# A conditioned hybrid decoder layer on one core: x in four loads, factor products spread out, five tiles of x1 turned by a transpose, and seven constant matmuls

## The chip, the core and the metric

The kernel runs on one NeuronCore of a Trainium2 chip. The metric is the device time of one execution in microseconds (us), the median of several runs; lower is better. One more execution was recorded by the hardware profiler, and all durations below come from it.

The engines are named as the profile names them: PE (matmul), PEld (its weight loads), DVE (vector), ACT (activation), POOL, and SP, which here only issues loads. Each works through its own list of instructions in order and waits at an instruction until what it needs is there.

## What is computed

One decoder layer for 256 tokens of width 2048 and a final norm, all in float32, with weights of some 380 MB read once:

```
mod = silu(c) W_ada + b_ada -> shift1, scale1, gate1, shift2, scale2, gate2
h   = RMSNorm(x)(1+scale1)+shift1
p   = h W_in                        (12288 columns: retention, HGRN2, two branch gates)
yA  = W_retO( LN_head(Retention(rope(q),rope(k),v)) * silu(g) )
yB  = W_hgO( RMS_head(HGRN2(silu(q), f, i)) * silu(g) )
x   = x + gate1 * ( (sigmoid(gA)*yA + sigmoid(gB)*yB) W_out )
h2  = RMSNorm(x)(1+scale2)+shift2
u   = causal_depthwise_conv3(h2 W_up) ; [a, b] = split(u)
x   = x + gate2 * ( (silu(a) * b) W_down )
out = RMSNorm_final(x)
```

## The kernel before

**Products.** A float32 weight piece of two k-tiles (128 x 1024, 512 KB) is loaded into `raw` (12 buffers), ACT copies its upper part to `wh` (`upper`, L165), DVE subtracts to get the lower part `wl` (`rest`, L170); both have four buffers. Activations are split alike: `hT` and `h2T` hold 256 upper and 256 lower columns for each k-tile. PE then forms hi x hi, lo x hi and hi x lo.

**The start (0 to about 43 us).** `load_x` (L268) brings x transposed in eight loads of 256 KB on SP's queue. `norm_x` (L312) squares them, two on DVE and six on ACT, with the four silu of c between ACT's squares, and adds them up on DVE. `token_rstd` (L282) sums over partitions with PE, takes the square root on ACT and the reciprocal on DVE, and spreads the result `rx` with two more matmuls. For each k-tile `scale_shift` (L386) makes scale and shift of the norm by four long products on DVE (`ada_dot`, L380: 1024 columns of W_ada times `sc`, summed). `times` (L367) multiplies x by `rx` in place; `modulated` (L337) makes the upper half of `hT` on ACT, the same value again as `h` on ACT, and the lower half by a subtraction on DVE. `run` does this by hand for the k-tiles 0 and 1, against four groups of columns (FIRST), and hands the other 14 to a background list (`ada[2:]`), from which `pump` takes steps in proportion to the products issued. Their seven `times` (512 columns each, k = 2, 4, ... 14) are tied only to an early instruction called `start`.

**Order.** Where `self.ordered` holds, `pin` keeps instructions in the order of the program text. Elsewhere a scheduler settles the order when the kernel is built. Either way each engine's list is fixed before the run.

**From x1 to h2T (about 785 to 822 us).** After the last group of W_out, `residual` (L875) adds to x1 and squares it, `row_rstd` (L893) gives a factor `rr` for each row, and `diag` (128 x 128) gets the factors on its diagonal. `turn_rows` (L345) multiplies 128 x 128 blocks of x1 by `diag` on PE, which turns and scales them at once. A tile of 512 columns holds two k-tiles of both row halves. The tiles j = 0, 1, 2 are turned first; `act2` (L852) turns j = 3 to 7 later, each ahead of the products that come one pair of k-tiles before its own. `modulated2` (L352) makes two k-tiles of `h2T` out of a tile in PSUM: on ACT the upper half of the first k-tile, `h` of the first, the upper half of the second; on DVE `h` of the second, then both subtractions. Then `up_group` (L900) runs the products with W_up: for each k-tile four matmuls of 512 columns (L913) and four of 256 (L915). One weight piece of W_up is prepared ahead of the last `residual`.

Of the kernel before, what the change touches and what calls it, by code (L numbers as in the profile page):

```python
# [55 lines left out]
class Kernel:  # L56
# [172 lines left out]
    def constants(self):  # L229
        nc, a, c = self.nc, self.a, self.consts  # L230
        self.ones = c.tile([P, P], F32, name="ones")
        nc.vector.memset(self.ones, 1.0)
        self.eps1 = c.tile([P, 1], F32, name="eps1")
        nc.vector.memset(self.eps1, NORM_EPS)
        self.eps2 = c.tile([P, 1], F32, name="eps2")
        nc.vector.memset(self.eps2, HEAD_EPS)
        self.halfpi = c.tile([P, 1], F32, name="halfpi")
        nc.vector.memset(self.halfpi, math.pi / 2)

        self.silu = []  # L240
        self.sc = c.tile([P, D + 1], F32, name="sc")
        nc.vector.memset(self.sc[:, D:], 1.0)
        rows = [self.blk([1, GW], name="crow") for _ in range(2)]
        for u, row in enumerate(rows):
            nc.scalar.dma_start(out=row, in_=a["c"][:, u * GW : (u + 1) * GW])
        self.small_loads(nc.scalar, ("ident", "gn1"))
        for u in range(4):
            at = slice(u * G, (u + 1) * G)
            ps = self.po()
            nc.tensor.matmul(ps, lhsT=self.ones[0:1, :], rhs=rows[u // 2][:, u % 2 * G : (u % 2 + 1) * G], start=True, stop=True)  # L250
            self.silu.append((self.sc[:, at], ps))

    def small_loads(self, engine, names):
        for name in names:
# [13 lines left out]
    def load_x(self):  # L268

        out = [self.blk([P, 4, T], name="xT") for _ in range(4)]  # L270
        for i in range(8):
            u = slice(i % 2 * 2, i % 2 * 2 + 2)
            self.pin(self.nc.sync.dma_start(out=out[i // 2][:, u, :], in_=self.a["xT"][:, 2 * i : 2 * i + 2, :]))
        return out

    def load_rows(self, j):
# [5 lines left out]
    def token_rstd(self, parts):  # L282


        nc = self.nc
        ps = self.po()[:, :NT]
        for i, z in enumerate(parts):
            for t in range(NT):

                nc.tensor.matmul(  # L290
                    ps[:, t : t + 1],
                    lhsT=z[:, t * P : (t + 1) * P],
                    rhs=self.ones[:, 0:1],
                    start=i == t == 0,
                    stop=i == len(parts) - 1,
                    skip_group_check=True,
                )
        q = self.small([P, NT], name="rq")
        nc.scalar.activation(q, ps, AF.Sqrt, bias=self.eps1, scale=1.0 / D)
        self.pin(nc.vector.reciprocal(q, q))  # L300

        ps = self.po()[:, :T]
        for t in range(NT):
            nc.tensor.matmul(ps[:, t * P : (t + 1) * P], lhsT=q[:, t : t + 1].to_broadcast([P, P]), rhs=self.ident, start=True, stop=True)
        return ps

    def sqrt_table(self):
# [4 lines left out]
    def norm_x(self):  # L312

        nc = self.nc
        self.xT = self.load_x()
        parts = []
        for i in range(8):
            x = self.xT[i // 2][:, i % 2 * 2 : i % 2 * 2 + 2, :]
            z = self.s2([P, 2, T], name="sq")
            if i < 2:  # L320
                nc.vector.tensor_tensor(z, x, x, ALU.mult)
            else:
                if self.silu:
                    self.pin(nc.scalar.activation(*self.silu.pop(0), AF.Silu))
                self.pin(nc.scalar.activation(z, x, AF.Square))
            if i % 2:
                nc.vector.tensor_tensor(z, z, last, ALU.add)
                if i % 4 == 3:
                    nc.vector.tensor_tensor(z[:, 0, :], z[:, 0, :], z[:, 1, :], ALU.add)
                    parts.append(z[:, 0, :])  # L330
                else:
                    parts += [z[:, 0, :], z[:, 1, :]]
            last = z
        self.sqrt_table()
        return parts

    def modulated(self, dst, x, k, sc, sh):  # L337

        act = self.nc.scalar.activation
        h = self.s1([P, T], name="h")  # L340
        self.pin(act(dst[:, :T], x, AF.Identity, bias=sh[:, k : k + 1], scale=sc[:, k : k + 1]))
        self.pin(act(h, x, AF.Identity, bias=sh[:, k : k + 1], scale=sc[:, k : k + 1]))
        self.pin(self.nc.vector.tensor_tensor(dst[:, T:], h, dst[:, :T].bitcast(F32), ALU.subtract))

    def turn_rows(self, ps, x, k, diag, t):  # L345

        for i in range(2):
            cols = slice((k + i) % 4 * P, ((k + i) % 4 + 1) * P)
            at = slice((NT * i + t) * P, (NT * i + t + 1) * P)
            self.pin(self.nc.tensor.matmul(ps[:, at], lhsT=x[k // 4][:, t, cols], rhs=diag[:, t, :], start=True, stop=True))  # L350

    def modulated2(self, dst, ps, k, sc, sh):  # L352

        nc = self.nc
        z = ps.rearrange("p (j t) -> p j t", j=2)
        hs = [self.s1([P, T], name="h") for _ in range(2)]
        for i, h in enumerate(hs):
            j = k + i
            self.pin(nc.scalar.activation(dst[:, i, :T], z[:, i, :], AF.Identity, bias=sh[:, j : j + 1], scale=sc[:, j : j + 1]))
            if i:  # L360
                self.pin(nc.vector.tensor_scalar(h, z[:, i, :], sc[:, j : j + 1], sh[:, j : j + 1], ALU.mult, ALU.add))
            else:
                self.pin(nc.scalar.activation(h, z[:, i, :], AF.Identity, bias=sh[:, j : j + 1], scale=sc[:, j : j + 1]))  # L363
        for i, h in enumerate(hs):
            self.pin(nc.vector.tensor_tensor(dst[:, i, T:], h, dst[:, i, :T].bitcast(F32), ALU.subtract))  # L365

    def times(self, k, n, r):  # L367
# [289 lines left out]
    def run(self):  # L657
# [12 lines left out]
        def act(k):  # L670
            return hT[k // 2][:, k % 2, :]

        def ada1(k):
            yield from self.scale_shift("ada1", k, s1, t1, self.gn1)
            if k % 2 == 0:
                hT[k // 2] = self.blk([P, 2, 2 * T], F32R, name="hT")
                if k:
                    ins = self.times(k, 2, rx_sb)
                    self.tc.add_manual_dep(ins.ins, start.ins.name, NOSYNC, reason="after the start")
            self.modulated(act(k), self.xT[k // 4][:, k % 4, :], k, s1, t1)  # L680
            yield 0.7

# [11 lines left out]


        ada = [ada1(k) for k in range(KT)]
        for _ in range(2):
            next(ada[0])
        rx = self.token_rstd(parts)
        rx_sb = c.tile([P, T], F32, name="rx_sb")  # L700
        ps = [self.po2(), self.po2(), self.pg(), self.pg()][:FIRST]
        for k in range(2):
            for i in range(4 if k else 2):
                if i == 1:
                    self.times(k, 1, rx)
                next(ada[k])
            part = self.upper(a["wa"][0][:, k : k + 1, :], 1, G)
            for _ in ada[k]:
                pass
            for g in range(FIRST):  # L710
                wh, wl = self.rest(part if g == 0 else self.upper(a["wa"][g][:, k : k + 1, :], 1, G))
                if k == 0:
                    start = self.last
                if k == g == 0:
                    self.pin(nc.scalar.activation(rx_sb, rx, AF.Copy))
                mms[g](ps[g], act(k), wh[:, 0, :], wl[:, 0, :], k == 0, k == 1 and g >= RESIDENT)
# [109 lines left out]
        for j in range(4):  # L826
# [4 lines left out]
            if last:  # L831
                self.finish(ada2)
                up = self.pieces(a["wup"][0], KT)
                up = chain([next(up)], up)
                self.ordered = True
            if last:
                diag = self.s1([P, NT, P], name="diag")
            for t in range(NT):
                self.residual(x1[j], ps, g, ss, j, t)
                if last:  # L840
                    r = self.row_rstd(ss, part, t)
                    self.pin(nc.vector.tensor_scalar(diag[:, t, :], self.ident, r, None, ALU.mult))
            if j == 2:
                part = self.row_part(ss)
# [6 lines left out]

        def act2(k):  # L852

            while len(h2T) < KT // 2 and 2 * len(h2T) <= k + 2:
                j = len(h2T)
                if j >= len(turned):
                    turned.append(self.po())
                    for t in range(NT):
                        self.turn_rows(turned[j], x1, 2 * j, diag, t)
                h2T.append(self.blk([P, 2, 2 * T], F32R, name="h2T"))  # L860
                self.modulated2(h2T[j], turned[j], 2 * j, self.sc2, self.sh2)
            return h2T[k // 2][:, k % 2, :]
# [206 lines left out]
```

## Time and profile before

| what | value |
|---|---|
| runs | 1540.33, 1540.42, 1541.73 us; median 1540.42 |
| profiled execution | 1540.23 us |
| its span, first to last instruction | 1538.3 us |
| outside the span | 1.9 us |
| mean granted PE clock | 0.999 |
| read from HBM | 382 MB, 250 GB/s over the span |

How to read it: the span is cut into stretches of time, and for each the profile tells how long every engine was busy. In a stretch where PE is busy all the time, nothing else can shorten the time but less work for PE. Where PE was idle, the table of waits tells what ended its idle time.

### The profile page before, as it was taken

Reading aid. Unit: us, or ns where it says so; the run is one execution under the profiler, and the core shown is the slowest. Engines: PE = TensorE matmul, PEld = TensorE weight load, DVE = VectorE, ACT = ScalarE, POOL = GpSimd, SP = SyncE. Lnnn points to the kernel's source line nnn. Section 1 sums busy time; section 2 is a strip of 40 time slices with the busy share of each in tenths; the row PEclk is TensorE's granted clock in tenths of the full one; section 3 lists DMA queues with packets and bytes.
Section 4 is the critical chain, followed back from the end, with each engine's and each line's share of the span. In section 5 each row is a group of like instructions: output and inputs, shape, how many; then the busy total and the mean of one; then the engine's idle time right before and its main releaser. Section 6 shows DMA issues by size and latency. Waiting matters only on the chain.

```text
span 1538.3 us, 22200 instructions
## 1 busy us (share of the span) xinstructions
PE 1516.6 (99%) x8286; PEld 1308.0 (85%) x8286; DVE 1173.4 (76%) x1595; ACT 843.4 (55%) x1201; POOL 4.0 (0%) x8
## 2 busy tenths in 40 slices
PE   7999999999999999999999999999999999999997
PEld 6999999888888888888878888888888888888886
DVE  7899986897998977898757787777778769455454
ACT  5755454766865554445446555555555558444343
POOL 0000000000000000000000000000000000000000
PEclk9999999999999999999999999999999999999999
DMA  9999997687777789989946777777777766677651
GB/s 362 346 345 329 319 330 228 232 280 256 247 246 261 262 293 322 320 303 342 337 121 216 226 232 233 240 222 239 230 231 232 226 189 190 206 207 206 198 166 55
DMA packets 111568, 385.69 MB, mean 251 GB/s; under 512 B 12866, under 2 KB 13410, under 8 KB 111460
## 3 DMA queue, kind: packets, MB, share of 16 engines
q1 hardware_dynamic: 110592, 383.14, 76.0%
q8 instruction: 65, 1.06, 0.3%
q10 hardware_dynamic: 868, 1.13, 0.2%
q14 instruction: 43, 0.35, 0.1%
HBM read 382.11 MB, written 2.11 MB: 250 GB/s over the span
## 4 chain that ended last, share of the span: by engine, by line
PE 94%; DVE 3%; ACT 2%; DMA 1%; issue 1%; DVEq 0%; ACTq 0%
PE pg L188 13%; PE pg L187 13%; PE pg L189 13%; PE po L913 11%; PE pg L913 10%; PE po L915 5%; PE pg L915 5%; PE po L189 3%; PE po L188 3%; PE po L187 3%; PE pg L202 3%; PE pg L200 3%; PE pg L201 3%; PE po L556 1%; DVE raw L380 1%; PE po L200 1%
## 5 line engine op out<-in xcount | busy, mean ns | idle before, releaser
L170 DVE TENSOR_TENSOR wl<-raw,wh 128x1024 fp32r<-128x1024 f32 (+1 forms) x536 | 635.0, 1189 | 283.3 <-ACT wh L165 281.9
L165 ACT ACTIVATE wh<-raw 128x1024 fp32r<-128x1024 f32 (+1 forms) x536 | 550.9, 1033 | 529.9 <-PE pg L189 190.4
L380 DVE SCALAR_TENSOR_TENSOR raw<-raw,sc 128x1024 f32<-128x1024 f32 x192 | 233.2, 1217 | 0.0
L913 PE MATMUL pg<-h2T,wh 128*128 128x512 f32 x704 | 221.6, 396 | 1.7 <-DVE h2T L365 1.7
L913 PE MATMUL po<-h2T,wh 128*128 128x512 f32 x704 | 221.2, 395 | 0.2 <-ACT wh L165 0.2
L187 PE MATMUL pg<-wh,hT 128*128 128x512 f32 x512 | 202.6, 396 | 0.0
L188 PE MATMUL pg<-wl,hT 128*128 128x512 f32 x512 | 200.2, 391 | 0.7 <-DVE wl L170 0.7
L189 PE MATMUL pg<-wh,hT 128*128 128x512 f32 x512 | 199.8, 390 | 0.0
L915 PEld LDWEIGHTS pg<-h2T,wl 128*128 128x128 f32 x704 | 131.9, 188 | 31.7 <-DVE wl L170 0.8
L915 PEld LDWEIGHTS po<-h2T,wl 128*128 128x128 f32 x704 | 132.2, 188 | 31.1
L915 PE MATMUL pg<-h2T,wl 128*128 128x256 f32 x704 | 138.5, 278 | 0.0
L915 PE MATMUL po<-h2T,wl 128*128 128x256 f32 x704 | 138.3, 278 | 0.0
L188 PEld LDWEIGHTS pg<-wl,hT 128*128 128x128 f32 x512 | 96.3, 188 | 21.1 <-DVE wl L170 2.3
L189 PEld LDWEIGHTS pg<-wh,hT 128*128 128x128 f32 x512 | 96.1, 188 | 20.2
L187 PEld LDWEIGHTS pg<-wh,hT 128*128 128x128 f32 x512 | 96.2, 188 | 19.1
L202 PE MATMUL pg<-hT,wl 128*128 128x256 f32 x384 | 109.0, 284 | 0.8 <-DVE wl L170 0.8
L200 PE MATMUL pg<-hT,wh 128*128 128x256 f32 x384 | 109.3, 285 | 0.1
L201 PE MATMUL pg<-hT,wh 128*128 128x256 f32 x384 | 109.0, 284 | 0.0
L913 PEld LDWEIGHTS pg<-h2T,wh 128*128 128x128 f32 x704 | 107.2, 189 | 1.8 <-ACT h L363 1.8
L913 PEld LDWEIGHTS po<-h2T,wh 128*128 128x128 f32 x704 | 107.2, 189 | 0.7 <-ACT wh L165 0.6
L200 PEld LDWEIGHTS pg<-hT,wh 128*128 128x128 f32 x384 | 74.1, 193 | 0.9 <-ACT wh L165 0.6
L202 PEld LDWEIGHTS pg<-hT,wl 128*128 128x128 f32 x384 | 74.0, 193 | 1.0 <-DVE wl L170 1.0
(222 smaller groups left out, 2198.4 us busy)
## 6 DMA issues: line engine op xcount, KB each, us to landing
raw<-in_wup SPq DMA_DIRECT2D x176, 512.0 KB, 4.5
raw<-in_wdown SPq DMA_DIRECT2D x88, 512.0 KB, 3.6
raw<-in_wa SPq DMA_DIRECT2D x80, 512.0 KB, 5.6
raw<-in_ada SPq DMA_DIRECT2D x64, 512.5 KB, 5.6
raw<-in_ada SPq DMA_DIRECT2D x64, 512.0 KB, 5.7
raw<-in_wab SPq DMA_DIRECT2D x64, 512.0 KB, 4.8
raw<-in_gate SPq DMA_DIRECT2D x32, 512.5 KB, 4.9
raw<-in_wb SPq DMA_DIRECT2D x32, 512.0 KB, 5.2
```

The source lines that it names most:

```text
L165: self.pin(self.nc.scalar.activation(wh, raw, AF.Copy))
L170: self.last = self.nc.vector.tensor_tensor(wl, raw, wh.bitcast(F32), ALU.subtract)
L187: nc.tensor.matmul(ps[t], lhsT=hi, rhs=wh, start=first, stop=False)
L188: nc.tensor.matmul(ps[t], lhsT=hi, rhs=wl, start=False, stop=False)
L189: nc.tensor.matmul(ps[t], lhsT=lo, rhs=wh, start=False, stop=last)
L200: nc.tensor.matmul(out, lhsT=wh[:, cs], rhs=hi, start=opens, stop=False, skip_group_check=True)
L201: nc.tensor.matmul(out, lhsT=wh[:, cs], rhs=lo, start=False, stop=False, skip_group_check=True)
L202: nc.tensor.matmul(out, lhsT=wl[:, cs], rhs=hi, start=False, stop=last, skip_group_check=True)
L380: dot = self.pin(nc.vector.scalar_tensor_tensor(raw[:, 0, :], raw[:, 0, :], 1.0, self.sc[:, u * GW : u * GW + w], ALU.mult, ALU.mult, accu ...
L556: nc.tensor.matmul(ps[:, j * 64 : (j + 1) * 64], lhsT=(kt if n > 1 else k)[:, h, c * P : (c + 1) * P], rhs=eq[:, j * 64 : (j + 1) * 64], s ...
L913: self.pin(nc.tensor.matmul(ps[j + z], lhsT=wh[:, cs[z]], rhs=act, start=kt == 0, stop=False))
L915: nc.tensor.matmul(ps[j + z][:, :T], lhsT=wl[:, cs[z]], rhs=act[:, :T], start=False, stop=kt == KT - 1)
```

## The change

**Start.** x comes in four loads of 512 KB. The first is squared on DVE, the other three on ACT in one instruction each, into buffers of a larger pool; two silu now come behind the last square. For k = 0 `modulated` makes `h` on DVE. The seven `times` of the background list stand at the head of a pair's steps and are tied to the newest `rest` (`self.last`). Matmuls of a block of ones in bfloat16 (`keep_busy`, 512 columns each) stand between steps of PE: two among the matmuls that spread c, three behind the sums of squares, two behind the spreading of `rx`.

**x1.** The tiles j = 0, 1, 2 are still turned with `diag`. For j = 3 to 7 DVE first scales x1 by the row factors into `xs` (two instructions of 256 columns), and four PE transposes turn `xs` (`turn_scaled`). `act2` does this one pair of k-tiles earlier. In `modulated2` DVE's `h` belongs to the first k-tile, ACT's to the second. Two weight pieces of W_up are prepared ahead, not one.

```
@@ constants
+        self.busy = self.sb.tile([P, G], BF16, name="busy", tag="k1", bufs=7)
+        nc.gpsimd.memset(self.busy, 1.0)
+        self.spare = self.pg()[0]
...
+            if u == 2:
+                self.keep_busy(2)
...
+    def keep_busy(self, n):
+
+        for _ in range(n):
+            self.pin(self.nc.tensor.matmul(self.spare, lhsT=self.busy[:, :P], rhs=self.busy, start=True, stop=True))
@@ load_x
-        for i in range(8):
-            u = slice(i % 2 * 2, i % 2 * 2 + 2)
-            self.pin(self.nc.sync.dma_start(out=out[i // 2][:, u, :], in_=self.a["xT"][:, 2 * i : 2 * i + 2, :]))
+        for i, z in enumerate(out):
+            self.pin(self.nc.sync.dma_start(out=z, in_=self.a["xT"][:, 4 * i : 4 * i + 4, :]))
@@ modulated
-        self.pin(act(h, x, AF.Identity, bias=sh[:, k : k + 1], scale=sc[:, k : k + 1]))
+        if k == 0:
+            self.pin(self.nc.vector.tensor_scalar(h, x, sc[:, k : k + 1], sh[:, k : k + 1], ALU.mult, ALU.add))
+        else:
+            self.pin(act(h, x, AF.Identity, bias=sh[:, k : k + 1], scale=sc[:, k : k + 1]))
@@ turn_scaled, new
+        z = self.s2([P, NT, 2 * P], name="xs")
+        for t in range(NT):
+            self.pin(self.nc.vector.tensor_scalar(z[:, t, :], x[:, t, :], rs[t], None, ALU.mult))
+        for t in range(NT):
+            for i in range(2):
+                at = slice((NT * i + t) * P, (NT * i + t + 1) * P)
+                self.pin(self.nc.tensor.transpose(ps[:, at], z[:, t, i * P : (i + 1) * P], self.ident))
@@ modulated2
             if i:
+                self.pin(nc.scalar.activation(h, z[:, i, :], AF.Identity, bias=sh[:, j : j + 1], scale=sc[:, j : j + 1]))
+            else:
                 self.pin(nc.vector.tensor_scalar(h, z[:, i, :], sc[:, j : j + 1], sh[:, j : j + 1], ALU.mult, ALU.add))
-            else:
-                self.pin(nc.scalar.activation(h, z[:, i, :], AF.Identity, bias=sh[:, j : j + 1], scale=sc[:, j : j + 1]))
-        for i, h in enumerate(hs):
             self.pin(nc.vector.tensor_tensor(dst[:, i, T:], h, dst[:, i, :T].bitcast(F32), ALU.subtract))
@@ ada1
+            if k > 0 and k % 2 == 0:
+                ins = self.times(k, 2, rx_sb)
+                self.tc.add_manual_dep(ins.ins, self.last.ins.name, NOSYNC, reason="behind the weights traced ahead of it")
...
-                if k:
-                    ins = self.times(k, 2, rx_sb)
-                    self.tc.add_manual_dep(ins.ins, start.ins.name, NOSYNC, reason="after the start")
@@ W_out, last group
-                up = chain([next(up)], up)
+                up = chain([next(up), next(up)], up)
@@ act2
-            while len(h2T) < KT // 2 and 2 * len(h2T) <= k + 2:
+            while len(h2T) < KT // 2 and 2 * len(h2T) <= k + 4:
...
-                    for t in range(NT):
-                        self.turn_rows(turned[j], x1, 2 * j, diag, t)
+                    self.turn_scaled(turned[j], x1[j // 2][:, :, j % 2 * 2 * P : (j % 2 + 1) * 2 * P], rs)
```

What this does to the engines' lists is seen at three places. The line numbers in rows of the changed kernel are its own.

DVE between the products for k = 1 and the first piece of a new group (`dot` is a long product, `xT<-xT,rx_sb` a `times`, `wl` a lower weight part). Before:

```order
L380 SCALAR_TENSOR_TENSOR raw_284,dot_283<-raw_284,sc 128x1024
L370 TENSOR_TENSOR xT_95<-xT_95,rx_sb 128x512
L380 SCALAR_TENSOR_TENSOR raw_287,dot_283<-raw_287,sc 128x1025
L370 TENSOR_TENSOR xT_96<-xT_96,rx_sb 128x512 x2
L370 TENSOR_TENSOR xT_97<-xT_97,rx_sb 128x512
L343 TENSOR_TENSOR hT_200<-h_296,hT_200 128x256
L170 TENSOR_TENSOR wl_293<-raw_290,wh_292 128x512
```

and changed:

```order
L399 SCALAR_TENSOR_TENSOR raw_280,dot_279<-raw_280,sc 128x1024
L399 SCALAR_TENSOR_TENSOR raw_283,dot_279<-raw_283,sc 128x1025
L353 TENSOR_TENSOR hT_196<-h_292,hT_196 128x256
L170 TENSOR_TENSOR wl_289<-raw_286,wh_288 128x512
L170 TENSOR_TENSOR wl_312<-raw_309,wh_311 128x512
```

The four `times` have left this place; one comes ahead of the long products for k = 2, the other six later, one ahead of each pair's products.

ACT a little later, where the first group beyond the first six begins (`p<-pg` takes a finished PSUM pair, `t` is the shift for k = 2, `wh_435` before and `wh_431` changed is that new group's first piece). Before:

```order
L392 ACTIVATE s_135<-gn_85,s_135 128x1
L165 ACTIVATE wh_435<-raw_433 128x1024
L691 ACTIVATE p_144<-pg_393 128x1024
L394 ACTIVATE t_136<-dot_418 128x1
L165 ACTIVATE wh_465<-raw_463 128x512
L341 ACTIVATE hT_426<-xT_95,t_136,s_135 128x256
L342 ACTIVATE h_428<-xT_95,t_136,s_135 128x256
```

and changed:

```order
L411 ACTIVATE s_130<-gn_88,s_130 128x1
L413 ACTIVATE t_131<-dot_415 128x1
L710 ACTIVATE p_139<-pg_390 128x1024
L348 ACTIVATE hT_423<-xT_100,t_131,s_130 128x256
L352 ACTIVATE h_424<-xT_100,t_131,s_130 128x256
L165 ACTIVATE wh_431<-raw_429 128x1024
```

The new group's first piece moved behind the taking of the last PSUM pair and behind `hT` and `h` of k = 2.

DVE from x1 to h2T, at the tiles j = 3 and 4 (`po_7461` and `po_7497` before, `po_7435` and `po_7474` changed, are those tiles in PSUM). Before:

```order
L361 TENSOR_SCALAR h_7468<-po_7461,sc_137,sh_138 128x256
L365 TENSOR_TENSOR h2T_7466<-h_7467,h2T_7466 128x256
L365 TENSOR_TENSOR h2T_7466<-h_7468,h2T_7466 128x256
L170 TENSOR_TENSOR wl_7494<-raw_7491,wh_7493 128x1024
L361 TENSOR_SCALAR h_7504<-po_7497,sc_137,sh_138 128x256
```

and changed:

```order
L384 TENSOR_TENSOR h2T_7410<-h_7412,h2T_7410 128x256
L366 TENSOR_SCALAR xs_7436<-xr_6827,rr_7361 128x256
L366 TENSOR_SCALAR xs_7436<-xr_6827,rr_7370 128x256
L383 TENSOR_SCALAR h_7444<-po_7435,sc_132,sh_133 128x256
L384 TENSOR_TENSOR h2T_7443<-h_7444,h2T_7443 128x256
L384 TENSOR_TENSOR h2T_7443<-h_7445,h2T_7443 128x256
L170 TENSOR_TENSOR wl_7471<-raw_7468,wh_7470 128x1024
L366 TENSOR_SCALAR xs_7475<-xr_7009,rr_7361 128x256
L366 TENSOR_SCALAR xs_7475<-xr_7009,rr_7370 128x256
L383 TENSOR_SCALAR h_7483<-po_7474,sc_132,sh_133 128x256
```

The scaling for the tile j = 4 now stands in DVE's list behind the subtractions of the tile j = 3 and behind the weight piece for the k-tiles 4 and 5 (`wl_7471`). The scaling for j = 3 stands behind the subtractions of j = 2. On PE the four transposes of j = 3 stand ahead of the products of k = 2, those of j = 4 ahead of k = 4, and so on to j = 7 ahead of k = 10; before, `turn_rows` for j = 3 stood ahead of k = 4, and for j = 7 ahead of k = 12.

More of the change, by code (lines that the diff above doesn't have):

```diff
@@ L249, in constants @@
             ps = self.po()
-            nc.tensor.matmul(ps, lhsT=self.ones[0:1, :], rhs=rows[u // 2][:, u % 2 * G : (u % 2 + 1) * G], start=True, stop=True)
+            if u == 2:
+                self.keep_busy(2)
+            self.pin(nc.tensor.matmul(ps, lhsT=self.ones[0:1, :], rhs=rows[u // 2][:, u % 2 * G : (u % 2 + 1) * G], start=True, stop=True))
             self.silu.append((self.sc[:, at], ps))
+    def keep_busy(self, n):
+        for _ in range(n):
+            self.pin(self.nc.tensor.matmul(self.spare, lhsT=self.busy[:, :P], rhs=self.busy, start=True, stop=True))
     def small_loads(self, engine, names):
@@ L288, in token_rstd @@
             for t in range(NT):
-                nc.tensor.matmul(
+                self.pin(nc.tensor.matmul(
                     ps[:, t : t + 1],
@@ L296, in token_rstd @@
                     skip_group_check=True,
-                )
+                ))
+        self.keep_busy(3)
         q = self.small([P, NT], name="rq")
@@ L303, in token_rstd @@
         for t in range(NT):
-            nc.tensor.matmul(ps[:, t * P : (t + 1) * P], lhsT=q[:, t : t + 1].to_broadcast([P, P]), rhs=self.ident, start=True, stop=True)
+            self.pin(nc.tensor.matmul(ps[:, t * P : (t + 1) * P], lhsT=q[:, t : t + 1].to_broadcast([P, P]), rhs=self.ident, start=True, stop=True))
+        self.keep_busy(2)
         return ps
@@ L316, in norm_x @@
         parts = []
[L317 to L321, printed above, removed]
+        for i, x in enumerate(self.xT):
+            z = self.blk([P, 4, T], name="sq")
+            if i == 0:
+                self.pin(nc.vector.tensor_tensor(z, x, x, ALU.mult))
             else:
-                if self.silu:
+                if i < 3:
                     self.pin(nc.scalar.activation(*self.silu.pop(0), AF.Silu))
                 self.pin(nc.scalar.activation(z, x, AF.Square))
[L326 to L330, printed above, removed]
-                else:
-                    parts += [z[:, 0, :], z[:, 1, :]]
-            last = z
+            self.pin(nc.vector.tensor_tensor(z[:, :2, :], z[:, :2, :], z[:, 2:, :], ALU.add))
+            self.pin(nc.vector.tensor_tensor(z[:, 0, :], z[:, 0, :], z[:, 1, :], ALU.add))
+            parts.append(z[:, 0, :])
+        for part in self.silu:
+            self.pin(nc.scalar.activation(*part, AF.Silu))
         self.sqrt_table()
@@ L350, in turn_rows, with turn_scaled @@
             self.pin(self.nc.tensor.matmul(ps[:, at], lhsT=x[k // 4][:, t, cols], rhs=diag[:, t, :], start=True, stop=True))
+    def turn_scaled(self, ps, x, rs):
+        z = self.s2([P, NT, 2 * P], name="xs")
[5 more added lines that the diff above has]
+                self.pin(self.nc.tensor.transpose(ps[:, at], z[:, t, i * P : (i + 1) * P], self.ident))
     def modulated2(self, dst, ps, k, sc, sh):
@@ L360, in modulated2 @@
             if i:
+                self.pin(nc.scalar.activation(h, z[:, i, :], AF.Identity, bias=sh[:, j : j + 1], scale=sc[:, j : j + 1]))
+            else:
                 self.pin(nc.vector.tensor_scalar(h, z[:, i, :], sc[:, j : j + 1], sh[:, j : j + 1], ALU.mult, ALU.add))
-            else:
-                self.pin(nc.scalar.activation(h, z[:, i, :], AF.Identity, bias=sh[:, j : j + 1], scale=sc[:, j : j + 1]))
-        for i, h in enumerate(hs):
             self.pin(nc.vector.tensor_tensor(dst[:, i, T:], h, dst[:, i, :T].bitcast(F32), ALU.subtract))
@@ L696, in run @@
         ada = [ada1(k) for k in range(KT)]
-        for _ in range(2):
+        for _ in range(3):
             next(ada[0])
@@ L702, in run @@
         for k in range(2):
-            for i in range(4 if k else 2):
-                if i == 1:
+            for i in range(4 if k else 1):
+                if k and i == 1:
                     self.times(k, 1, rx)
                 next(ada[k])
+            if k == 0:
+                self.times(k, 1, rx)
             part = self.upper(a["wa"][0][:, k : k + 1, :], 1, G)
@@ L711, in run @@
                 wh, wl = self.rest(part if g == 0 else self.upper(a["wa"][g][:, k : k + 1, :], 1, G))
-                if k == 0:
-                    start = self.last
                 if k == g == 0:
@@ L837, in run @@
                 diag = self.s1([P, NT, P], name="diag")
+                rs = []
             for t in range(NT):
@@ L841, in run @@
                     r = self.row_rstd(ss, part, t)
+                    rs.append(r)
                     self.pin(nc.vector.tensor_scalar(diag[:, t, :], self.ident, r, None, ALU.mult))
```

## The prediction

> **What bounds the kernel now.** I read the page first, then the span cut into stretches, then the waits of PE, then the rows of time where PE waits. The page's head and its first list:
>
> ```profile
> span 1538.3 us, 22200 instructions
> ...
> PE 1516.6 (99%) x8286; PEld 1308.0 (85%) x8286; DVE 1173.4 (76%) x1595; ACT 843.4 (55%) x1201; POOL 4.0 (0%) x8
> ```
>
> The stretches give the start, the length and the busy time of PE, PEld, DVE, ACT and POOL in that order, then the granted clock, the DMA share and GB/s:
>
> ```profile
> 0.00:14.00 14.00, 11.55 (x29) 6.95 (x30) 5.42 (x14) 8.18 (x13) 0.20 (x4) 1.00 0.88 297
> 14.00:42.00 28.00, 22.50 (x128) 20.24 (x128) 26.33 (x45) 15.42 (x29) 0.00 (x0) 1.00 1.03 401
> 42.00:500.00 458.00, 456.42 (x2890) 409.48 (x2890) 399.44 (x531) 278.07 (x397) 3.83 (x4) 1.00 0.83 284
> 500.00:766.00 266.00, 266.00 (x1211) 220.58 (x1210) 217.14 (x272) 134.15 (x180) 0.00 (x0) 1.00 0.91 313
> 766.00:830.00 64.00, 60.41 (x336) 51.30 (x335) 40.20 (x64) 38.35 (x63) 0.00 (x0) 1.00 0.49 152
> 830.00:1480.00 650.00, 650.00 (x3482) 558.66 (x3481) 459.22 (x644) 349.83 (x500) 0.00 (x0) 1.00 0.72 219
> ```
>
> PE is the bound, with hardly a gap from 42 to 766 and from 830 to 1480. There only less work for PE could help, and the change takes none away. So only two places count: the start, where DVE is busy 26.33 of the 28 us from 14 to 42, and the passage from x1 to h2T, where PE idles 3.59 us between 766 and 830. PE never catches up later on: what it loses at one of these places is lost for good, and what it gains is kept. PE's waits between 786 and 830 (the engine and line that waited, what for, us in total, times, longest):
>
> ```profile
> PE pg L913 <- DVE h2T L365: 1.7, 1, 1.7
> PE po L350 <- DVE diag L842: 1.3, 1, 1.3
> ```
>
> Both lie ahead of the first product of W_up. After it, the five later `turn_rows` cost PE their own work and almost no waiting.
>
> **From x1 to h2T: the term that decides.** Rows of time of before (start, duration, engine, line, operation):
>
> ```profile
> 791.84 0.56 ACT L359 ACTIVATE h2T<-po,sh,sc 128x256 fp32r<-128x256 f32 x1 [1.32 <-PE po L350]
> ...
> 793.81 0.75 DVE L365 TENSOR_TENSOR h2T<-h,h2T 128x256 fp32r<-128x256 f32 x2
> ...
> 794.37 0.70 PE L913 MATMUL pg<-h2T,wh 128*128 128x512 f32 x2 [1.68 <-DVE h2T L365]
> ...
> 795.85 1.22 DVE L170 TENSOR_TENSOR wl<-raw,wh 128x1024 fp32r<-128x1024 f32 x1
> ...
> 797.03 0.54 DVE L361 TENSOR_SCALAR h<-po,sc,sh 128x256 f32<-128x256 f32 x1
> ...
> 800.02 1.06 PE L350 MATMUL po<-diag,xr 128*128 128x128 f32 x8
> 800.83 0.71 PE L913 MATMUL pg<-h2T,wh 128*128 128x512 f32 x2
> 801.11 0.56 ACT L359 ACTIVATE h2T<-po,sh,sc 128x256 fp32r<-128x256 f32 x1 [3.17 <-PE po L350]
> ...
> 801.58 0.55 ACT L363 ACTIVATE h<-po,sh,sc 128x256 f32<-128x256 f32 x1
> ...
> 802.03 0.56 ACT L359 ACTIVATE h2T<-po,sh,sc 128x256 fp32r<-128x256 f32 x1
> ...
> 802.48 1.06 ACT L165 ACTIVATE wh<-raw 128x1024 fp32r<-128x1024 f32 x1
> 802.62 0.55 DVE L361 TENSOR_SCALAR h<-po,sc,sh 128x256 f32<-128x256 f32 x1 [3.24 <-ACT h2T L359]
> ...
> 815.70 0.71 PE L913 MATMUL pg<-h2T,wh 128*128 128x512 f32 x2
> ```
>
> PE's own price: 794.37 to 800.02 is four k-tiles, 1.41 each. A turn takes 0.81 (800.02 to 800.83). From 800.83 to 815.70 are four turns and eight k-tiles, 3.72 a loop, so before hardly waits.
>
> The new order of `modulated2` has the two engines hand one PSUM tile over: ACT `h2T`, DVE `h`, ACT `h2T`, ACT `h`. In before, DVE's `h` starts at 802.62, 0.03 after ACT's second `h2T` ends (802.59): a reader on the other engine waits for the first. I take the same for ACT's second `h2T` behind DVE's `h`. Then a tile holds ACT for 0.59 + 0.57 + 0.46 + 0.46 = 2.08, against 1.37 before (801.11 to 802.48). Before shows the wait in this one direction only. The Trainium skill, "PSUM — Partial Sum Buffer", section "PSUM bank collisions raise a hardware error", says that the compiler orders any two instructions of different engines on the same bank and partitions, reads against reads too. By that rule the new order pays 0.57 more per tile, as I have it; without it the change would be some 4.5 us cheaper (the third rival's sum, made from the rows).
>
> Start: the first `h` is on DVE at 791.84 + 0.59 and done by 792.89, the subtraction 0.56 later (793.81 to 794.37 is that step): the first product comes at 793.45, a gain of 0.92. Two k-tiles then keep PE to 796.27, and there stand, new, the transposes of j = 3.
>
> They need `xs`, which stands in DVE's list behind the subtractions of j = 2. That tile's ACT work starts at 791.84 + 2 x 2.08 = 796.00, its `h` on ACT ends 1.62 later, the subtraction, priced by 793.81 (0.75 for two), ends near 798.25. Transposes and scaling are priced by like rows elsewhere, four transposes on PE and a scaling of 512 columns on DVE:
>
> ```profile
> 669.36 0.60 PE L469 MATMUL po<-ident,gt 128*128 128x128 f32 x4
> ...
> 669.71 0.48 PE L187 MATMUL pg<-wh,og 128*128 128x512 f32 x1
> ...
> 1527.31 1.28 DVE L977 TENSOR_SCALAR xr<-xr,rr 128x512 f32<-128x512 f32 x3
> ```
>
> Transposes: 0.35 for four. Scaling: 0.40 from one to the next at 512 columns (three in 1.28); at 256 I estimate 0.27, between 0.20 and 0.40. So the second `xs` ends near 798.9 and the transposes start at 798.98: PE has waited 2.7 us.
>
> The loop from one tile's last transposes to the next's is then a circle through three engines: transposes to ACT 0.45, `h2T` 0.59, DVE's `h` 0.57, ACT's `h2T` 0.46 and `h` 0.46, then ACT's `wh` 1.09 (802.48), DVE's `wl` 1.18 (795.85 to 797.03), first `xs` 0.27, second `xs` to PE 0.43. Sum 5.50. PE has only 2 x 1.41 + 0.35 = 3.17 for it, so it waits 2.3 a loop; before had 3.72 and no such circle, since `turn_rows` read x1 and a `diag` long finished. Four loops bring the transposes of j = 7 to 798.98 + 22.0 = 820.98; with them and k = 10, 11 done, 824.15. The weights for k = 12, 13 are late too: `wl` is there 4.85 after the transposes, PE wants it at 3.17 + 0.47: 1.2 more. The same point of the work in before is 815.70. **Sum: 825.35 - 815.70 = +9.65** for this part, 8.0 if the estimates of `xs` and of the first tiles are all favourable, 11.5 with each step 0.1 longer. The five lighter turns save PE 5 x 0.46 = 2.3 of work, already in the sum, but PE waits there anyway. The second prepared piece of W_up is counted at nothing: ACT and DVE are free ahead of the residual; without that cover it would be 1.1 + 1.2.
>
> **The start.** The loads of x, from issue to landing, in before:
>
> ```profile
> DMA to landing us min/median/max: 3.0/5.2/6.3
> ```
>
> Rows of time of before: a square on ACT, two early products on PE, three of the four rows that hold the seven `times` on DVE, and the end of the first six groups:
>
> ```profile
> 11.44 1.15 ACT L325 ACTIVATE sq<-xT 128x512 f32<-128x512 f32 x2 [0.68 <-PE po L290]
> ...
> 24.57 0.41 PE L200 MATMUL pg<-hT,wh 128*128 128x256 f32 x1
> 24.79 0.41 PE L201 MATMUL pg<-hT,wh 128*128 128x256 f32 x1
> ...
> 27.03 0.68 DVE L370 TENSOR_TENSOR xT<-xT,rx_sb 128x512 f32<-128x512 f32 x1
> ...
> 28.78 1.88 DVE L370 TENSOR_TENSOR xT<-xT,rx_sb 128x512 f32<-128x512 f32 x3
> ...
> 36.24 1.28 DVE L370 TENSOR_TENSOR xT<-xT,rx_sb 128x512 f32<-128x512 f32 x2
> ...
> 40.98 1.04 ACT L165 ACTIVATE wh<-raw 128x1024 fp32r<-128x1024 f32 x1
> ...
> 42.08 0.39 PE L200 MATMUL pg<-hT,wh 128*128 128x256 f32 x1
> ...
> 42.16 1.02 ACT L691 ACTIVATE p<-pg 128x1024 f32<-128x1024 f32 x1
> ...
> 43.79 0.59 ACT L341 ACTIVATE hT<-xT,t,s 128x256 fp32r<-128x256 f32 x1
> ...
> 44.28 0.59 ACT L342 ACTIVATE h<-xT,t,s 128x256 f32<-128x256 f32 x1
> ```
>
> Six of the seven `times` leave DVE's chain, 0.60 each (36.24): 3.6, less 0.3 for the `h` it takes over. Earlier squares may add 0 to 2.5 (two silu of 0.6 now stand behind them on ACT, but both ahead of the square root that follows): the 0.68 wait for a buffer goes, but x is the same bytes in four loads as in eight on SP's queue, and their landing (3.0 to 6.3 us after issue) bounds the rest. I take the end of the six groups 3.7 earlier than 42.08, between 1.5 and 5.8. But the next group's first piece now stands on ACT behind `p` (1.02), `hT` and `h` (0.49 each, 43.79 to 44.28) and takes 1.04 itself: 3.04 of PE idle, where before had that piece from 40.98. Net -0.65. The six `times` that come later cost +0.15, between 0 and 0.3: from 42 to 500 DVE is busy 399 of 458 us, so there is slack to take 3.6. **Sum: -0.5**, from -2.8 to +1.5. The constant matmuls: 24.57 to 24.79 is 0.22 for 256 columns, against 1.41/12 = 0.12 in the later k-tiles, so PE is slow until about 26, though the granted clock reads 1.00. From the first products at about 20 on that is 6/0.22, some 27 of them, so a fast PE would save up to 27 x 0.10 = 2.6 of its work, but DVE's long products set `hT` for k = 1; I count 0. The Trainium skill, "TensorE: Matmul & The Clock Gate", Part 1, asks for about 3.4 us of sustained work before the clock opens. Seven such matmuls, in three pieces, are by its rule too short (an estimate: 7 x 0.43 = 3.0), so the sum by it is the same 0.
>
> **Sum.** 1540.23 - 0.5 + 9.65 = 1549.4 for a profiled execution; the median of the runs is 0.2 above it, so 1549.6.
>
> **Rivals.** *The scaled blocks never hold PE up* (faster): then the first product's 0.92 and five turns at 0.46 are gained, with 0.5 of the start: 1540.4 - 3.7 = 1536.7. It speaks for it that ACT is busy 38 and DVE 40 of 64 us: there is room on average. Against it, `xs` stands in line behind `wl`, and `wl` behind ACT's `wh`. It decides at a loop of 3.17; I have 5.50. Chance 0.06.
>
> *The clock falls while PE waits*: at 0.215 per 256 columns a k-tile takes 2.58, a loop 5.8, and k = 10 to 13 some 4 more: about 1554.5. Against it, the waits of 1.3 and 1.7 left the granted clock of 766 to 830 at 1.00, and those I forecast are up to 2.7. Chance 0.05.
>
> *ACT and DVE read the tile at once*: 0.57 less in three first tiles, four loops and the end, 4.5 in all: 1545.1. Against it the 0.03 at 802.62. Chance 0.06.
>
> *The change does less than it says after x1 and more at the start*: that last case, with the start at its best end and a PE that the constant matmuls make fast: 1545.1 - 2.3 - 2.6 = 1540.2. Chance 0.03.
>
> **How the numbers follow.** The forecast keeps 0.80. Its own range is 1540.4 + 8.0 - 2.8 = 1545.6 to 1540.4 + 11.5 + 1.5 = 1553.4, ends that need all at once; with the third rival at the lower end I give 1545.0 to 1553.0. About 0.2% (3 us) is what a measurement can tell from no change: faster is the first rival, 0.06; same the last, 0.03; slower the rest, 0.91.
>
> **What would show it.** In the profile after, PE's waits for a transpose on `xs` should total about 12 us in five pieces (the first near 2.7, the others near 2.3), ACT's second `h2T` should start about 0.03 after DVE's `h` ends, and the first product of W_up should come 0.9 sooner after the first turn's end. At the start, `wh` of the seventh group should hold PE about 3 us. I am wrong if PE is busy through the first group of W_up, if `xs` starts before `wl`, or if ACT's and DVE's reads overlap.

## The result and the profile after

The changed kernel is slower: 1552.06 us (median of 5 runs, 1550.63 to 1552.31) against 1540.42; ratio 1.0069, 95% interval 1.0058 to 1.0081. The profiled execution took 1552.06 us, its span 1550.2 against 1538.3 before: 11.9 us longer. The stretches of the changed kernel, cut as before but with the passage from x1 to h2T 12 us longer (PE, PEld, DVE, ACT, POOL busy, granted clock, DMA share, GB/s):

```profile
14.00:42.00 28.00, 23.09 (x132) 19.57 (x131) 20.86 (x37) 15.65 (x30) 0.00 (x0) 0.94 1.03 407
42.00:500.00 458.00, 455.14 (x2879) 409.07 (x2880) 400.49 (x528) 276.70 (x388) 3.83 (x4) 1.00 0.83 281
...
766.00:842.00 76.00, 64.89 (x328) 54.07 (x327) 46.82 (x75) 40.27 (x65) 0.00 (x0) 0.96 0.45 141
842.00:1492.00 650.00, 650.00 (x3482) 558.55 (x3481) 459.13 (x644) 349.73 (x499) 0.00 (x0) 1.00 0.71 219
```

The row of 766 to 842 carries most of it. From 842 on PE is busy all of 650 us with 3482 matmuls, the row of 830 to 1480 of before, 12 us later. Where 64 us stood, 76 stand now, and PE is idle 11.1 us in them instead of 3.6. Some 2.3 of these 12 us come from the start: the first turn behind the second `diag` begins that much later (rows below). In 14 to 42 DVE is down from 26.33 to 20.86 us busy, so the start did unload DVE, and the granted clock is 0.94. The waits of PE over the whole execution:

```profile
PE po L370 <- DVE xs L366: 7.5, 5, 2.4
PE pg L200 <- ACT wh L165: 3.0, 1, 3.0
PE po L200 <- ACT hT L348: 2.7, 2, 2.4
...
PE pg L935 <- DVE wl L170: 0.5, 1, 0.5
...
PE pg L933 <- ACT wh L165: 0.4, 1, 0.4
```

The two top waits are those forecast: five for `xs`, and one of 3.0 for the seventh group's first piece. The five add up to 7.5 us, though, where about 12 had been forecast. Two of them are only 0.5, because PE ran slowly ahead of them (below). The other three are 2.39, 2.07 and 2.05, where 2.7 and 2.3 had been forecast: the profile counts a wait from the end of the last product, some 0.2 later than PE could have begun the next one, and the loop itself is as long as forecast. One turn of the circle, from the transposes of one tile to the next, in the rows of time of the changed kernel:

```profile
806.81 0.63 PE L370 MATMUL po<-ident,xs 128*128 128x128 f32 x4 [0.49 <-DVE xs L366]
...
807.48 0.57 ACT L379 ACTIVATE h2T<-po,sh,sc 128x256 fp32r<-128x256 f32 x1 [2.33 <-PE po L370]
...
808.08 0.54 DVE L383 TENSOR_SCALAR h<-po,sc,sh 128x256 f32<-128x256 f32 x1 [1.15 <-ACT h2T L379]
...
808.66 0.57 ACT L379 ACTIVATE h2T<-po,sh,sc 128x256 fp32r<-128x256 f32 x1 [0.61 <-DVE h L383]
...
809.12 0.56 ACT L381 ACTIVATE h<-po,sh,sc 128x256 f32<-128x256 f32 x1
...
809.57 1.06 ACT L165 ACTIVATE wh<-raw 128x1024 fp32r<-128x1024 f32 x1
...
810.66 1.23 DVE L170 TENSOR_TENSOR wl<-raw,wh 128x1024 fp32r<-128x1024 f32 x1 [0.52 <-ACT wh L165]
811.80 0.61 DVE L366 TENSOR_SCALAR xs<-xr,rr 128x256 f32<-128x256 f32 x2
812.30 0.63 PE L370 MATMUL po<-ident,xs 128*128 128x128 f32 x4 [2.07 <-DVE xs L366]
```

Read downwards, each row starts where the one above lets it, across three engines: 806.81 to 812.30 is 5.49 us (forecast 5.50). ACT's second `h2T` waits for DVE's `h` and starts 0.04 after it ends (808.08 + 0.54 = 808.62), so the tile is handed over in both directions.

### The profile page after: what moved, and what is told of

Read it like the earlier page. It is cut to its first block, busy times and chain, and to the rows that moved or that the text cites. A ratio compares the mean times of both kernels' runs of the same rounds, so it can differ in the third digit from the quotient of the medians.

```text
span 1550.2 us, 22158 instructions
## 1 busy us (share of the span) xinstructions
PE 1520.0 (98%) x8265; PEld 1308.0 (84%) x8265; DVE 1179.8 (76%) x1607; ACT 845.5 (55%) x1197; POOL 4.6 (0%) x9
## 3 DMA queue, kind: packets, MB, share of 16 engines
q8 instruction: 65, 1.06, 0.3%
## 4 chain that ended last, share of the span: by engine, by line
PE 92%; ACT 2%; DVE 2%; DMA 1%; issue 0%; DVEq 0%; ACTq 0%
PE pg L187 13%; PE pg L188 13%; PE pg L189 13%; PE po L933 11%; PE pg L933 10%; PE po L935 5%; PE pg L935 5%; PE po L189 3%; PE pg L202 3%; PE po L187 3%; PE po L188 3%; PE pg L200 3%; PE pg L201 3%; PE po L575 1%; PE po L202 1%; PE po L201 1%
```

## The experiments

Ratios are to the kernel before, timed on the same chip, with 95% intervals.

**The two parts apart.** `x1_only` is before with the x1 part, `start_only` the changed kernel with that part undone; `modulated2` goes with the x1 part in both.

```
x1_only, against before:
-                up = chain([next(up)], up)
+                up = chain([next(up), next(up)], up)
-            while len(h2T) < KT // 2 and 2 * len(h2T) <= k + 2:
+            while len(h2T) < KT // 2 and 2 * len(h2T) <= k + 4:
-                    for t in range(NT):
-                        self.turn_rows(turned[j], x1, 2 * j, diag, t)
+                    self.turn_scaled(...)
...
start_only, against the changed kernel:
-            while len(h2T) < KT // 2 and 2 * len(h2T) <= k + 4:
+            while len(h2T) < KT // 2 and 2 * len(h2T) <= k + 2:
-                    self.turn_scaled(...)
+                    for t in range(NT):
+                        self.turn_rows(turned[j], x1, 2 * j, diag, t)
-                up = chain([next(up), next(up)], up)
+                up = chain([next(up)], up)
...
```

> The kernel before with only the x1 part of the change (scaled blocks for tiles 3 to 7, one pair earlier, the new order of modulated2, two prepared pieces). My theory: all but about 2 us of the loss lies here; the circle transposes - ACT - DVE - ACT - wh - wl - xs costs 5.5 us a loop, so 1540.4 + 9.65 = 1550, and PE's transposes wait for xs five times. Rival: the two parts work on each other (the later start of W_up with other weights in flight), and the part alone costs under 7 us.

> The changed kernel with the x1 part undone: only the new start. My theory from the trace: first products 2.2 us sooner, but the piece of the seventh group stands behind p, hT and h on ACT and PE waits 3.0 us and then runs slowly for a while, so this part alone is slower: 1540.4 + 2.2 = 1542.6. Rival: the start gains 0.5 as predicted (1539.9) and the 2.3 us at 791 come from somewhere else.

Measured: `x1_only` 1550.52, ratio 1.0061 (1.0045 to 1.0078), that is +9.4 us, and its span is 9.7 over that of before. `start_only` 1542.11, ratio 1.0002 (0.9993 to 1.0012), +0.3 us, between -1.1 and +1.8. Together 1.0063, within the interval of the whole change, so the parts add up and the x1 part is nearly all of the loss. The +2.2 that I expected of `start_only`, from one profiled execution, is not what its runs give. Its profiled execution is again 2.2 longer than the profiled one of before: more on that below. The turns in `x1_only`, where nothing of the start is changed:

```profile
798.82 0.70 PE L360 MATMUL po<-ident,xs 128*128 128x128 f32 x4 [2.39 <-DVE xs L356]
804.38 0.63 PE L360 MATMUL po<-ident,xs 128*128 128x128 f32 x4 [2.06 <-DVE xs L356]
809.86 0.63 PE L360 MATMUL po<-ident,xs 128*128 128x128 f32 x4 [2.06 <-DVE xs L356]
815.34 0.63 PE L360 MATMUL po<-ident,xs 128*128 128x128 f32 x4 [0.51 <-DVE xs L356]
820.82 1.08 PE L360 MATMUL po<-ident,xs 128*128 128x128 f32 x4 [2.06 <-DVE xs L356]
```

Forecast were 798.98 for the first and 820.98 for the last.

**The circle cut.** `ahead` is the changed kernel with the scaling of the next tile on DVE ahead of the work on this tile.

```
                    self.turn_scaled(turned[j], xs[j])
+                if 2 <= j < KT // 2 - 1:
+                    xs[j + 1] = self.scaled(...)
                 h2T.append(...)
                 self.modulated2(...)
```

> The changed kernel, but the two scalings of the next tile stand on DVE ahead of the work on this tile, so no xs stands behind a wl. If the circle through xs and wl is the cause, PE's waits for xs go and this part of the program comes out near or below before: 1552.1 - 9.65 - 1.6 = about 1541, between 1540 and 1544. Rival: ACT's time for a tile, lengthened by the hand-over of the PSUM tile (2.08 + 1.06 for wh = 3.14 a loop), is the bound of its own and most of the loss stays, over 1547.

Measured: 1545.08, ratio 1.0025 (1.0016 to 1.0035), so 0.0044 or 6.8 us better than the changed kernel, yet above the 1544 expected. PE's waits in `ahead` from 786 to 830:

```profile
PE pg L943 <- DVE wl L170: 2.1, 4, 0.5
...
PE pg L941 <- ACT wh L165: 1.3, 1, 1.3
...
PE po L374 <- DVE xs L366: 0.3, 1, 0.3
```

The waits for `xs` have gone from 7.5 to 0.3. In their place PE waits 3.4 for `wh` and `wl`: with tiles turned a pair earlier, the weight piece that PE needs next stands behind two tiles' work on ACT. After these waits PE ran slowly for some 3 us here too (from 805.75 on, 1.06 for two products of 512 columns). My expectation had counted only part of this.

**The hand-over.** `old_mod` is the changed kernel with `modulated2` as before; the circle stays.

```
             if i:
-                self.pin(nc.scalar.activation(h, z[:, i, :], AF.Identity, ...))
-            else:
                 self.pin(nc.vector.tensor_scalar(h, z[:, i, :], ...))
+            else:
+                self.pin(nc.scalar.activation(h, z[:, i, :], AF.Identity, ...))
+        for i, h in enumerate(hs):
             self.pin(nc.vector.tensor_tensor(dst[:, i, T:], h, ..., ALU.subtract))
```

> The changed kernel with the order of before in modulated2 (ACT makes both parts of the first k-tile, DVE the h of the second), the circle through xs and wl left in. My theory: the hand-over between ACT and DVE is one term of the circle; without it wl can start 0.5 us sooner after the transposes, a loop takes about 5.0 instead of 5.5, and with the first three tiles 3 to 4.5 us come back: 1547.5 to 1549. Rival: the hand-over is hidden beside the circle and the time stays within 1 us of the changed kernel's.

Measured: 1547.55, ratio 1.0040 (1.0024 to 1.0055). Against the changed kernel the medians differ by 4.5 us, on two chips; in the profiled executions, from the first turn behind the second `diag` to the second product of k = 12, by 4.1. Two turns of its circle:

```profile
800.34 0.70 PE L370 MATMUL po<-ident,xs 128*128 128x128 f32 x4 [0.23 <-DVE xs L366]
...
805.35 0.63 PE L370 MATMUL po<-ident,xs 128*128 128x128 f32 x4 [1.50 <-DVE xs L366]
...
810.29 0.63 PE L370 MATMUL po<-ident,xs 128*128 128x128 f32 x4 [1.51 <-DVE xs L366]
```

805.35 to 810.29 is 4.94: the hand-over was 0.55 of each turn, and PE's wait is 1.5 where it was 2.07.

**The x1 part mended.** `mended` is before with scaled blocks and transposes, but with nothing of the circle: the scaling one tile ahead, the turns one pair of k-tiles ahead as before, each weight piece prepared one ahead, the new `modulated2` for the first tile only (`early` makes a list of pieces run one ahead).

```
+                if 2 <= j < KT // 2 - 1:
+                    xs[j + 1] = self.scaled(...)
...
-                    for t in range(NT):
-                        self.turn_rows(turned[j], x1, 2 * j, diag, t)
+                    self.turn_scaled(turned[j], xs[j])
...
+                up = early(up)
                 up = chain([next(up)], up)
...
-            if i:
+            if (i == 0) == (k == 0):
```

> The kernel before with the x1 part mended: scaled blocks for tiles 3 to 7, the scaling one tile ahead, the turns again one pair of k-tiles ahead, each weight piece prepared one ahead, the new order of modulated2 for the first tile alone. If only the circle and the hand-over made the loss, the transposes now gain: 0.8 at the first product and 5 x 0.46 at the turns, so 3 us under before, ratio 0.998. Rival: DVE's work for a pair (xs 0.6, h 0.55, two subtractions 0.85, wl 1.2 = 3.2 us) is as long as PE's 3.17 and eats the gain, ratio 0.999 to 1.000.

Measured: 1538.07, ratio 0.9980 (0.9971 to 0.9988), 3.1 us faster. PE's waits in `mended` from 786 to 830, and three rows of time:

```profile
PE po L359 <- DVE diag L871: 1.3, 1, 1.3
PE pg L945 <- DVE h2T L388: 0.9, 1, 0.9
...
```

```profile
803.85 0.60 PE L373 MATMUL po<-ident,xs 128*128 128x128 f32 x4
...
807.09 0.60 PE L373 MATMUL po<-ident,xs 128*128 128x128 f32 x4
...
810.32 0.60 PE L373 MATMUL po<-ident,xs 128*128 128x128 f32 x4
```

No wait is left between the turns, and a loop is 3.23 to 3.24, close to PE's own 3.17 and to DVE's work for a pair, where it was 3.72 before. So transposes of scaled blocks are worth their 0.46 a turn; what stood around them made them cost, and most of it was the place of the scaling in DVE's list.

**The start.** `old_times` is the changed kernel with the seven `times` tied to the first pieces again; `start_old_times` is that start with x1 as before; `start_no_busy` leaves the seven constant matmuls out too.

```
old_times, against the changed kernel:
-            if k > 0 and k % 2 == 0:
-                ins = self.times(k, 2, rx_sb)
-                ... behind self.last
+                if k:
+                    ins = self.times(k, 2, rx_sb)
+                    ... behind start
start_no_busy, besides:
-            self.keep_busy(2)
-        self.keep_busy(3)
-        self.keep_busy(2)
```

> The changed kernel with the multiplications by the norm factor tied as before: in the built order the piece of the seventh group stands on ACT ahead of p and hT again, and five of the multiplications stand between the long products of k = 1 and the first small pieces. If the 3.0 us wait comes from the order on ACT, it goes and the time falls by 1 to 3 us: about 1550. Rival: the multiplications back in DVE's chain delay the products of k = 1 by as much (0.6 each, 3 us), and nothing is gained or 1 us is lost.

> The new start alone, x1 as before, but the multiplications by the norm factor tied as before. My theory: the order on ACT (the seventh group's piece behind p, hT and h) cost the new start its gain; without it the new start is 2 us faster than before, ratio 0.9985. Rival: the gain seen in the kernel with both parts was of the clock's chance, ratio 1.000 or above.

> The same as the run before it but without the seven constant matmuls. My theory: they make PE's first products run at full clock (0.28 for 256 columns instead of 0.41) but DVE sets the pace there, so leaving them out costs under 0.5 us. Rival: they carry 2 us or more of the start, and without them the time is that of before or more.

Measured: `old_times` 1.0048 (1.0033 to 1.0063) against 1.0069 (1.0058 to 1.0081) with the new tie; `start_old_times` 0.9991 (0.9982 to 1.0000) against 1.0002 (0.9993 to 1.0012). Both pairs differ the same way, by 0.0021 and 0.0011, though their intervals overlap. The wait of 3.0 for the seventh group's piece is in the traces of all four kernels with the whole new start (the changed one, `start_only`, `ahead`, `old_mod`) and in none of those with the old tie. In `old_times` ACT makes that piece at 39.94, ahead of `h` (40.89), `p` (41.55) and `hT` (42.47) again, so the ACT order makes the wait. `start_no_busy` has 0.9986 (0.9977 to 0.9994): without the constant matmuls the start is not slower, and rather 0.8 us faster, a difference that these intervals don't separate.

**Both mended.** The mended x1 part and the start of the last two runs in one kernel, without and with the constant matmuls.

```
both_mended: mended + start_no_busy
both_mended_busy: mended + start_old_times
```

> The mended x1 part together with the new start without its constant matmuls and with the multiplications tied as before. If the two parts are independent, as the sum of the parts alone says, the gains add: 0.998 x 0.9986 = 0.9966, about 1536. Rival: the gain of one is eaten by the other (weights that arrive later, a slow stretch of PE), ratio 0.998.

> The same with the seven constant matmuls. If they bring nothing, the ratio is that of the run before it or up to 0.0005 higher (0.9966 to 0.9971). Rival: they keep the clock up where it counts and the time is 1 us lower.

Measured: 1535.29, ratio 0.9961 (0.9949 to 0.9974), and 1536.24, ratio 0.9966 (0.9954 to 0.9978). The gains add. The first is 6.3 us faster than before on its chip and beats both kernels; the constant matmuls again bring nothing that the intervals show.

## Why the prediction was right, and where it was not

**The x1 part was right in mechanism and in size.** +9.65 was forecast; the part alone is 9.7 longer in its profiled execution and 9.4 in the ratio, and in the changed kernel 11.9 less the 2.26 of the start (below) leaves 9.6. `ahead` shows that the scaling behind `wl` is the main cause: with the scaling moved and all else kept the waits for `xs` go, and 6.8 us come back. `old_mod` shows the hand-over as one term of the circle. The third rival priced the hand-over at 4.5; `old_mod`, which undoes the earlier first product as well, gave back 4.5 by the medians and 4.1 by the profile. As the rule on PSUM banks in the Trainium skill ("PSUM — Partial Sum Buffer", section "PSUM bank collisions raise a hardware error") has it, DVE's `h` between two of ACT's reads serializes them: the 0.04 at 808.62 shows the second direction, which the trace of before did not. The first product came 1.75 after the tile's first `h2T` (794.10 to 795.85), 2.53 before: a gain of 0.78, not 0.92. The sum had given DVE's `h` 0.46 there, and it took 0.58 (794.70 to 795.28).

**The clock rival's condition came true, its price did not.** In two of the four loops PE ran slowly in the changed kernel (the granted clock from 766 to 842 is 0.96, and was 1.00 in the passage of before). Rows of time of the second:

```profile
813.57 0.63 PE L935 MATMUL pg<-h2T,wl 128*128 128x256 f32 x2
814.00 1.05 PE L933 MATMUL pg<-h2T,wh 128*128 128x512 f32 x2
...
817.77 0.63 PE L370 MATMUL po<-ident,xs 128*128 128x128 f32 x4 [0.51 <-DVE xs L366]
```

Two products of 512 columns take 1.05 instead of 0.63, and the wait that follows is 0.51 instead of 2.07. The loop, 812.30 to 817.77, is 5.47 all the same: the slow products fit into the wait. The rival's price assumed that a slow PE would be the bound for a whole loop; it was slow for some 3.6 us of one at a time.

**The start is where the sum was off.** Forecast was -0.5, from -2.8 to +1.5 (by its own terms the upper end is +1.8). By the runs it is +0.3 (-1.1 to +1.8), in the range; in the profiled executions it is +2.26, outside. The first turn behind the second `diag`, in the changed kernel and in before:

```profile
793.35 1.60 PE L360 MATMUL po<-diag,xr 128*128 128x128 f32 x12 [1.30 <-DVE diag L863]
```

```profile
791.09 1.60 PE L350 MATMUL po<-diag,xr 128*128 128x128 f32 x12 [1.30 <-DVE diag L842]
```

The step that failed is "I take the end of the six groups 3.7 earlier than 42.08", and in it the term "Six of the seven `times` leave DVE's chain, 0.60 each". The end came 1.8 earlier (40.27). Rows of the changed kernel:

```profile
10.77 1.22 DVE L399 SCALAR_TENSOR_TENSOR raw<-raw,sc 128x1024 f32<-128x1024 f32 x1
...
17.19 0.60 ACT L348 ACTIVATE hT<-xT,t,s 128x256 fp32r<-128x256 f32 x1 [0.74 <-DVE xT L389]
...
26.58 0.51 PE L200 MATMUL po<-hT,wh 128*128 128x256 f32 x2 [2.39 <-ACT hT L348]
...
27.97 0.41 PE L200 MATMUL po<-hT,wh 128*128 128x256 f32 x1
...
34.65 0.40 PE L187 MATMUL pg<-wh,hT 128*128 128x512 f32 x1
...
40.31 1.02 ACT L710 ACTIVATE p<-pg 128x1024 f32<-128x1024 f32 x1
41.23 0.59 ACT L348 ACTIVATE hT<-xT,t,s 128x256 fp32r<-128x256 f32 x1
41.73 0.59 ACT L352 ACTIVATE h<-xT,t,s 128x256 f32<-128x256 f32 x1
42.22 3.03 ACT L165 ACTIVATE wh<-raw 128x1024 fp32r<-128x1024 f32 x4
...
43.31 0.38 PE L200 MATMUL pg<-hT,wh 128*128 128x256 f32 x1 [3.04 <-ACT wh L165]
...
45.20 0.41 PE L202 MATMUL pg<-hT,wl 128*128 128x256 f32 x1
```

and of before, the first long product, the first `hT` and the same two products of PE:

```profile
13.69 1.22 DVE L380 SCALAR_TENSOR_TENSOR raw<-raw,sc 128x1024 f32<-128x1024 f32 x1
...
19.39 0.60 ACT L341 ACTIVATE hT<-xT,t,s 128x256 fp32r<-128x256 f32 x1
...
29.87 0.50 PE L200 MATMUL po<-hT,wh 128*128 128x256 f32 x2 [0.86 <-ACT hT L341]
...
36.50 0.40 PE L187 MATMUL pg<-wh,hT 128*128 128x512 f32 x1
```

The products of k = 1 did come forward, by 29.87 - 26.58 = 3.3, but hardly by the `times`. 2.2 of it is there with the first `hT` already (19.39 to 17.19): the squares are done sooner, and DVE begins its long products at 10.77 instead of 13.69. 0.5 lies between this `hT` and DVE's next long product (3.87 before, 3.38 now), where DVE now makes `h` itself. 0.6 is a single `times`, that of 27.03, the only one of the seven that stood ahead of a long product for k = 1. With all seven back, in `old_times`, the products of k = 1 begin at 27.48, 0.9 later, or 1.2 counted from the first product of k = 0. The forecast had 3.3 for the `times` and 0.4 for the squares, so that its sum came near the 3.3 was luck.

Then PE lost part of it. It had done the products of k = 0 earlier still, so it waited 2.39 for `hT` instead of 0.86, and then ran at 0.41 instead of 0.28 for 17 products. At the first product of the next group 1.85 was left (36.50 - 34.65). The wait on ACT's order took 3.04, as forecast to the hundredth. The seventh group began 1.23 late, and then PE ran slowly again for 15 products. I had counted the end of the slow stretch of before as worth nothing, and had not counted that new ones can follow a longer wait.

The seven constant matmuls were counted at 0, and the runs without them agree. In the changed kernel PE's first products take 0.28 from 18.9 on, in `start_only`, which has the same start, 0.41 until 21.8, and yet the products of k = 1 begin at 26.58 and 26.66: DVE sets the pace there, as the prediction said.

## What to carry to other kernels

When work moves from the engine that is full to one that seems free, write down the whole circle from one tile to the next with every engine's list in order: here a circle of 5.5 us stood against 3.2 us of PE's work, though DVE and ACT were busy only 47 and 40 of the 76 us. The first repair was to move the scaling in DVE's list, so that the operand of the next tile is made before the work on this tile. Alone it gave back 6.8 us and left the kernel slower than before; a gain came when the turns, the weight pieces and the hand-over were put right with it. What makes the next tile's operand should not be handed from ACT to DVE and back within one PSUM tile where something waits for it.

## What the runs showed of the hardware

A wait of PE can be followed by a stretch of slow products, and its length alone doesn't settle whether it is. In the changed kernel the wait of 2.39 for the first `xs` was followed by slow products, so that only 0.49 was left of the next wait; in `x1_only` the same 2.39 was not, and the next wait is 2.06. `mended` has the start of before unchanged, and yet in its profiled execution, after a wait of 1.47 where before had 0.86, products run slowly where those of before did not:

```profile
29.70 0.50 PE L209 MATMUL po<-hT,wh 128*128 128x256 f32 x2 [1.47 <-ACT hT L350]
...
33.95 0.41 PE L210 MATMUL po<-hT,wh 128*128 128x256 f32 x1
...
34.95 0.28 PE L211 MATMUL po<-hT,wl 128*128 128x256 f32 x1
```

Its first turn behind the second `diag` begins at 792.38, 1.3 later than in before. The 27 runs of before on the chip of `mended` lie between 1540.01 and 1542.99. The 13 of them under 1541 have a mean granted clock of 0.998 or 0.999, the 14 above it of 0.996 to 0.998, so the spread of 3 us goes with the clock; that the slow stretches make all of it is argued, not shown. It means that one profiled execution can't tell a change of 2 us in the start, and that its span of one kernel against another's can mislead by as much. The Trainium skill, "TensorE: Matmul & The Clock Gate", Part 1, has PE fall to half speed after an idle window of about 3.4 us, in windows that run freely; here waits of 1.5 to 3.0 us with short work around them were followed by slow stretches of 3 to 6 us in some executions and by none in others, and no run shows the windows. And the granted clock of a stretch doesn't always tell: from 20 to 26 before reads 1.00 while its products take 0.41.

Whether constant matmuls placed in the wait ahead of the products of k = 1 would keep PE fast was not tried.
